# A two-layer encoder trunk on one core: gates and branch projections with token tiles as the stationary operand, and a transpose of the merged sum

## The chip, the core and the metric

The kernel runs on one core of one Trainium2 chip. Its metric is device time in microseconds (us). Three runs of the kernel before took 1342.67, 1344.53 and 1344.79 us; the median is 1344.53 us.

## What is computed

Two layers (`DEPTH = 2`) over 256 tokens of 1024 channels, all in float32. Each layer projects the tokens to three token mixers (pooling A, attention B, a gated recurrence C) and to three gates, projects the mixers' outputs to the model width, merges them by the gates and projects once more:

```
proj = einsum('bsd,de->bse', x, w_in[i])
...
y_a = einsum('bsc,cd->bsd', multiscale_pool(a_in, ...), w_branch_a[i])          # 1024 -> 1024
y_b = einsum('bsc,cd->bsd', dilated_attention_mixer(...), w_branch_b[i])        #  512 -> 1024
y_c = einsum('bsc,cd->bsd', hgrn2_bidirectional(...), w_branch_c[i])            # 1024 -> 1024
gates = sigmoid(gate_raw).reshape(B, S, 3, D_MODEL)
merged = gates[:, :, 0] * y_a + gates[:, :, 1] * y_b + gates[:, :, 2] * y_c
x1 = layer_norm(ALPHA * x + merged @ w_out[i], ln1_g[i], ln1_b[i])
```

A SwiGLU feed-forward, a gated per-layer embedding and a second layer norm end the layer.

## The kernel before

**Products.** Every matrix product is made of three matmuls per pair of tiles (`mm3`, L246 to L250): both operands are held as a high part and a low part of float32r, and high times high, high times low and low times high are added in PSUM. There are two ways to lay a product out. `gemm_cols` (L252) takes 128 weight columns as the stationary operand (`lhsT`) and moves all 256 tokens past them: 128x256 per matmul, and the result has output channels on the partitions. `gemm_tok` (L268) takes 128 tokens as the stationary operand and moves 512 weight columns: 128x512 per matmul, tokens on the partitions; it goes through both tiles of tokens (t = 0, 1), each with all eight tiles of k.

**The weight stream.** All weights come as 1 MB pieces in one fixed order, the list `chunks` (L139 to L176): `cols` is 256 columns of all eight k tiles, `blk` is 512 columns of four k tiles, `rws` 256 whole rows. A piece is loaded (`raw`, SP's queue, L193), split on ScalarE into `whi` (L206) and on VectorE into `wlo` (L207), and used. Each of the three names has three buffers, so the split of piece n waits until piece n-3 has been used by TensorE. `use_chunk` takes the next split piece; `step_end` (L241) splits one more piece and lets some background work be issued.

**Order.** The helper tasks of attention, recurrence and pooling are Python generators that are run in slices by `background` (L221). The order on each engine is then made by a scheduler over the whole program, so the program's text gives only dependences and priorities; the rows of the built program show the order itself.

**The stage in question**, L718 to L785, once in each layer. It makes, for branch C, four times a gate product (`gemm_cols` with the residual stream `xh`, `xl`), `gate` (tanh on ScalarE, L724) and the branch product (with `oh`, `ol`); VectorE then multiplies gate and product out of PSUM into `mg` (`merge`, L730). The pooling product follows (L747 to L757). Then branch B (half as deep) and its gates, and four times branch A's gate and product, where `merge` multiplies (L732) and adds (L733). `mg` has channels on the partitions, which is the layout that the output projection wants for its stationary operand: L782 and L783 split it into `mh`, `ml` as it is finished, a quarter at a time. The projection itself is `rows_gemm` (L799): four pieces of two k tiles, the first two pieces used at once for both tiles of tokens, the last two held and used tile by tile.

`tbank` gives one of four PSUM banks named `t` (transposes and small products), `gbank` one of four named `g`. `s4`, `s5`, `s7`, `s8`, `sa`, `sb` are named SBUF slots with one buffer each: a new tile in a slot waits for the last reader of the old one. A transpose is a matmul against `ident`.

Of the kernel before, what the change touches and what calls it, by code (L numbers as in the profile page):

```python
# [30 lines left out]
# columns of the constants' array  # L31
# [47 lines left out]
def trunk(ctx: ExitStack, tc: tile.TileContext, x, p, w_in, pool_w, pool_scale, w_branch_a,  # L79
# [59 lines left out]
    for l in range(DEPTH):  # L139
# [19 lines left out]
        for c in range(2):  # L159
            blk(w_branch_b[l], 0, 512 * c)  # L160
            cols(w_in[l], C_GATE + 1024 + 512 * c)
            cols(w_in[l], C_GATE + 1024 + 512 * c + 256)
        for c in range(4):
            cols(w_in[l], C_GATE + 256 * c)
            cols(w_branch_a[l], 256 * c)
# [75 lines left out]
    def step_end():  # L241
        split_chunk()
        background()

# [23 lines left out]
    def gemm_tok(ws, act, evac, between):  # L268
        """512 output columns, both tiles of tokens, ws: two pieces of four k tiles."""
        for t in range(2):  # L270
            ps = gbank()
            for k in range(KD):
                w = ws[k // 4]
                mm3(ps, act(k, t), (w[0][:, k % 4, :], w[1][:, k % 4, :]), k == 0, k == KD - 1)
# [37 lines left out]
    def layer_norm(t, gb, ress, then):  # L312
        """ress: per half of the columns (base, scale or None, psum)."""
# [29 lines left out]
    def hgrn_task(l, hp, q, ff, kf, fb, kb, vt, gt, oh, ol):  # L343
# [14 lines left out]
        for d in range(2):  # L358
# [30 lines left out]
            # totals of the chunks of 32  # L389
# [6 lines left out]
            # blocks of 64 stand at 0, 2, 4; the one scaled to its tile's far end beside the middle one  # L396
# [16 lines left out]
            # scaled: fwd queries block 3 by total of 2, keys block 0 by total of 1; bwd mirrored  # L413
# [130 lines left out]
    def pool_task(g, a, mix):  # L544
        # a: [P, 2, 272], the channels' values between zeros
# [88 lines left out]
    for l in range(DEPTH):  # L634
        # token-major operands: the recurrence's values and gate
# [51 lines left out]
        # attention  # L687
# [30 lines left out]
        # gates and branches  # L718
        finish("hgrn")
        mg = slot("s4", [P, KD, S])  # L720

        def gate(ps):
            s = misc([P, 512])
            A.activation(out=s, in_=ps, func=AF.Tanh, scale=0.5)  # L724
            return s

        def merge(s, y, c, first):
            dst = mg[:, 2 * c:2 * c + 2, :].rearrange("p m t -> p (m t)")
            if first:
                V.scalar_tensor_tensor(out=dst, in0=s, scalar=1.0, in1=y, op0=ALU.add, op1=ALU.mult)  # L730
            else:
                V.scalar_tensor_tensor(out=s, in0=s, scalar=1.0, in1=y, op0=ALU.add, op1=ALU.mult)  # L732
                V.tensor_tensor(out=dst, in0=dst, in1=s, op=ALU.add)  # L733

        for c in range(4):
            ps = gbank()
            gemm_cols(use_chunk(), xk, ps)
            s = gate(ps)
            step_end()
            ps = gbank()  # L740
            gemm_cols(use_chunk(), lambda k: (oh[:, k, :], ol[:, k, :]), ps)
            merge(s, ps, c, True)
            step_end()
# [15 lines left out]
        for c in range(2):  # L759
            pb = [gbank(), gbank()]  # L760
            w = use_chunk()
            for i in range(2):
                gemm_cols(w, lambda k: (ob[:, 0, k, :], ob[:, 1, k, :]), pb[i], nk=4, m0=2 * i)
            step_end()
            for i in range(2):
                ps = gbank()
                gemm_cols(use_chunk(), xk, ps)
                merge(gate(ps), pb[i], 2 * c + i, False)
                step_end()
        mh, ml = None, None  # L770
        for c in range(4):
            ps = gbank()
            gemm_cols(use_chunk(), xk, ps)
            s = gate(ps)
            step_end()
            ps = gbank()
# [142 lines left out]
```

## Time and profile before

| what | value |
|---|---|
| runs, us | 1342.67, 1344.53, 1344.79 (median 1344.53) |
| span of the profiled execution, us | 1341.4 |
| busy share of the span: TensorE, its weight loads, VectorE, ScalarE, GpSimd | 98%, 92%, 65%, 44%, 1% |
| granted TensorE clock, 40 slices | 9 tenths or more of full speed in every slice |
| mean DMA rate | 174 GB/s |

The profiled execution has no time of its own beside its span; the span starts and ends with the first and last instruction that the profiler shows, and the median of the runs is 3.1 us above it. A row of a timeline begins with its start in us and its length in us; a group of instructions has its count, its total busy time and the mean length of one in ns. A matmul's length is from its start to its modelled end and overlaps with the next one, so what a matmul costs in a row of them is the distance from start to start.

### The profile page before, as it was taken

To read this page: it belongs to the slowest core of one execution; us is meant where nothing else is said; L and a number is where in the kernel's file an instruction comes from. 1 tells how busy PE (TensorE), PEld (TensorE's weight loads), DVE (VectorE), ACT (ScalarE), POOL (GpSimd) and SP (SyncE) were. 2 spreads that over 40 slices of the span, in tenths; PEclk is the share of its full clock that TensorE was granted. 3 is DMA by queue.
4 is the path that set the end of the run, shared out by engine and by line. 5 is a ranking of instruction groups with operands and counts; after the bars stand their busy time and mean duration, and the time that the engine had idled before them with its cause. 6 is when DMAs were issued, how large, how long until landed. Compare 5 with 4: busy or idle time off the path is not lost.

```text
span 1341.4 us, 22091 instructions
## 1 busy us (share of the span) xinstructions
PE 1317.5 (98%) x9609; PEld 1236.9 (92%) x9609; DVE 868.7 (65%) x1126; ACT 585.9 (44%) x644; POOL 16.6 (1%) x24
## 2 busy tenths in 40 slices
PE   8999999999999999999989999999999999999997
PEld 6899999999999799998779999999999997999986
DVE  4598888574655765544555999875746558544545
ACT  5444444553444444443334444455534444444431
POOL 0000000000000000000000000000000000000000
PEclk9999999999999999999999999999999999999999
DMA  8654544245556465655356554442455564765551
GB/s 309 200 178 158 178 138 161 93 156 181 176 186 219 158 221 188 189 186 190 127 184 196 179 164 158 158 158 95 159 168 186 188 216 142 239 188 183 179 195 40
DMA packets 180769, 233.56 MB, mean 174 GB/s; under 512 B 3841, under 2 KB 149825, under 8 KB 180673
## 3 DMA queue, kind: packets, MB, share of 16 engines
q1 hardware_dynamic: 178976, 227.44, 51.7%
q10 hardware_dynamic: 1696, 4.72, 1.1%
q8 instruction: 75, 1.23, 0.4%
q14 instruction: 22, 0.17, 0.0%
HBM read 231.10 MB, written 1.05 MB: 173 GB/s over the span
## 4 chain that ended last, share of the span: by engine, by line
PE 93%; DVE 4%; issue 1%; ACT 1%; POOL 1%; DMA 0%; POOLq 0%; DVEq 0%; ACTq 0%
PE g L248 29%; PE g L249 28%; PE g L250 28%; DVE wlo L207 2%; PE t L439 1%; PE t L426 1%; PE t L434 1%; PE t L307 1%; POOL rs_y L297 1%; PE t L523 1%; PE t L463 1%; PE t L464 1%; ACT whi L206 0%; DVE ln_st L321 0%; PE t L503 0%
## 5 line engine op out<-in xcount | busy, mean ns | idle before, releaser
L207 DVE TENSOR_TENSOR wlo<-raw,whi 128x2048 fp32r<-128x2048 f32 (+2 forms) x218 | 489.9, 2248 | 339.7 <-ACT whi L206 339.4
L206 ACT ACTIVATE whi<-raw 128x2048 fp32r<-128x2048 f32 (+2 forms) x218 | 410.0, 1883 | 566.7 <-issue 259.6
L248 PE MATMUL g<-xh,whi 128*128 128x256 f32 x1984 | 564.4, 284 | 0.0
L250 PE MATMUL g<-xh,wlo 128*128 128x256 f32 x1984 | 561.7, 283 | 0.0
L249 PE MATMUL g<-xl,whi 128*128 128x256 f32 x1984 | 561.6, 283 | 0.0
L248 PEld LDWEIGHTS g<-xh,whi 128*128 128x128 f32 x1984 | 380.7, 192 | 0.2
L249 PEld LDWEIGHTS g<-xl,whi 128*128 128x128 f32 x1984 | 380.7, 192 | 0.2
L250 PEld LDWEIGHTS g<-xh,wlo 128*128 128x128 f32 x1984 | 380.6, 192 | 0.0
L248 PE MATMUL g<-whi,xh 128*128 128x512 f32 x288 | 115.1, 400 | 1.2 <-ACT whi L206 1.2
L249 PE MATMUL g<-wlo,xh 128*128 128x512 f32 x288 | 114.6, 398 | 1.4 <-DVE wlo L207 1.4
L250 PE MATMUL g<-whi,xl 128*128 128x512 f32 x288 | 113.3, 395 | 0.0
L249 PEld LDWEIGHTS g<-wlo,xh 128*128 128x128 f32 x288 | 55.6, 193 | 14.1 <-DVE wlo L207 3.1
L248 PEld LDWEIGHTS g<-whi,xh 128*128 128x128 f32 x288 | 55.6, 193 | 13.7 <-ACT whi L206 1.8
L250 PEld LDWEIGHTS g<-whi,xl 128*128 128x128 f32 x288 | 55.4, 192 | 11.5
L248 PE MATMUL g<-s,whi 128*128 128x256 f32 x192 | 54.3, 283 | 0.0
L250 PE MATMUL g<-s,wlo 128*128 128x256 f32 x192 | 54.3, 283 | 0.0
L249 PE MATMUL g<-s,whi 128*128 128x256 f32 x192 | 54.3, 283 | 0.0
L249 PE MATMUL g<-wlo,s 128*128 128x512 f32 x128 | 50.1, 392 | 0.0
L250 PE MATMUL g<-whi,s 128*128 128x512 f32 x128 | 50.1, 391 | 0.0
L248 PE MATMUL g<-whi,s 128*128 128x512 f32 x128 | 49.6, 390 | 0.0
L865 DVE TENSOR_TENSOR m<-m,g 128x512 f32<-128x512 f32 x22 | 15.1, 687 | 36.9 <-PE g L250 36.9
L248 PE MATMUL g<-whi,sa 128*128 128x512 f32 x96 | 37.5, 391 | 0.0
(177 smaller groups left out, 1472.4 us busy)
## 6 DMA issues: line engine op xcount, KB each, us to landing
raw<-in_w_in_dram SPq DMA_DIRECT2D x106, 1024.0 KB, 5.1
raw<-in_w_ffn_gate_dram SPq DMA_DIRECT2D x22, 1024.0 KB, 5.4
raw<-in_w_ffn_up_dram SPq DMA_DIRECT2D x22, 1024.0 KB, 5.4
raw<-in_w_ffn_down_dram SPq DMA_DIRECT2D x22, 1024.0 KB, 4.8
raw<-in_w_branch_c_dram SPq DMA_DIRECT2D x8, 1024.0 KB, 5.0
raw<-in_w_branch_a_dram SPq DMA_DIRECT2D x8, 1024.0 KB, 5.0
raw<-in_w_out_dram SPq DMA_DIRECT2D x8, 1024.0 KB, 4.8
raw<-in_w_ple_gate_dram SPq DMA_DIRECT2D x8, 1024.0 KB, 5.1
```

Source lines behind the costliest of these rows:

```text
L206: A.activation(out=hi[:, ks, :], in_=t[:, ks, :], func=AF.Copy)
L207: V.tensor_tensor(out=lo[:, ks, :], in0=t[:, ks, :], in1=f(hi[:, ks, :]), op=ALU.subtract)
L248: PE.matmul(ps, lhsT=ah, rhs=bh, start=first, stop=False)
L249: PE.matmul(ps, lhsT=ah, rhs=bl, start=False, stop=False)
L250: PE.matmul(ps, lhsT=al, rhs=bh, start=False, stop=last)
L297: G.tensor_tensor(out=y, in0=v, in1=mhalf.to_broadcast([P, n]) if n > 1 else mhalf, op=ALU.pow)
L307: PE.transpose(ps[:, k * P:(k + 1) * P], xt[:, t, (4 * hf + k) * P:(4 * hf + k + 1) * P], ident)
L426: PE.matmul(dg[po:po + 64, co:co + 64], lhsT=KI[:, cs], rhs=QI[:, cs], start=True, stop=True)
L434: PE.matmul(cr[po:po + 64, co:co + 64], lhsT=KL[:, h, 4 * t, :], rhs=QL[:, h, 4 * t, :], start=True, stop=True)
L439: PE.matmul(lg[:, co:co + P], lhsT=kp.rearrange("p b u -> p (b u)"), rhs=qp.rearrange("p b u -> p (b u)"), start=True, stop=True)
L463: PE.matmul(o, lhsT=at[:, 2 * h + t, :], rhs=vt[:, t, hs], start=True, stop=False)
L865: V.tensor_tensor(out=s, in0=s, in1=pu.rearrange("p (m t) -> p m t", t=S), op=ALU.mult)
```

## The change

The list of pieces has `blk` in place of `cols` for the gates and for branches A and C, and a new order of pieces. The stage's products go through `tok_block` (`gemm_tok` with one or two pieces): for each half n of the 1024 output columns a block of gate products and a block of branch products. Gates now stay in the slots s5 (branch C), s7 (B) and s8 (A) until the branch product is there. `mg` has tokens on the partitions. `turn(n)` transposes half n of it on TensorE, eight transposes in two banks, and splits the banks into `mh`, `ml`; `turn(0)` is a background task of branch A's second half, `turn(1)` is issued within `rows_gemm` after its first piece. The rest of the program has the same instructions. Helper lines move by a few: mm3's matmuls are L252 to L254, the split L210 and L211, the gate L728, merges L739, L741 and L742, the attention's transposes L528, their copy out of PSUM L530, its products with the values L536 to L539, pooling's split L296 and L297, the transposes of `p` L802, the new transposes L777 and their split L780 and L781.

```diff
-        for c in range(4):
-            cols(w_in[l], C_GATE + 2048 + 256 * c)
-            cols(w_branch_c[l], 256 * c)
+        for n in range(2):
+            for k in range(2):
+                blk(w_in[l], 512 * k, C_GATE + 2048 + 512 * n)
+            for k in range(2):
+                blk(w_branch_c[l], 512 * k, 512 * n)
...
-    def tok_block(act, evac, between=None):
-        ws = [use_chunk(), use_chunk()]
+    def tok_block(act, evac, between=None, n=2):
+        ws = [use_chunk() for _ in range(n)]
         gemm_tok(ws, act, evac, between)
-        step_end()
-        step_end()
+        for _ in range(n):
+            step_end()
...
-        mg = slot("s4", [P, KD, S])
+        mg = slot("s4", [P, 2, D])
...
+        def branch(n, gates, act, first=False, pieces=2, then=None):
+            def ev_gate(t, ps):
+                gate(ps, gates[:, t, :])
+            def ev(t, ps):
+                s, dst = gates[:, t, :], mg[:, t, 512 * n:512 * n + 512]
+                if first:
+                    V.scalar_tensor_tensor(out=dst, in0=s, scalar=1.0, in1=ps, op0=ALU.add, op1=ALU.mult)
+                else:
+                    V.scalar_tensor_tensor(out=s, in0=s, scalar=1.0, in1=ps, op0=ALU.add, op1=ALU.mult)
+                    V.tensor_tensor(out=dst, in0=dst, in1=s, op=ALU.add)
+            tok_block(xtok, ev_gate)
+            tok_block(act, ev, n=pieces)
...
+        def turn(n):
+            for j in (2 * n, 2 * n + 1):
+                ps = tbank()
+                for k in range(2):
+                    for t in range(2):
+                        c0 = (2 * j + k) * P
+                        PE.transpose(ps[:, k * S + t * P:k * S + (t + 1) * P], mg[:, t, c0:c0 + P], ident)
+                ks = slice(2 * j, 2 * j + 2)
+                v = ps.rearrange("p (k t) -> p k t", t=S)
+                A.activation(out=mh[:, ks, :], in_=v, func=AF.Copy, scale=0.5)
+                V.scalar_tensor_tensor(out=ml[:, ks, :], in0=v, scalar=0.5, in1=f(mh[:, ks, :]),
+                                       op0=ALU.mult, op1=ALU.subtract)
...
-        rows_gemm(4, 2, lambda k, t: (mh[:, k, t * P:(t + 1) * P], ml[:, k, t * P:(t + 1) * P]), ln1)
+        finish("turn")
+        rows_gemm(4, 2, lambda k, t: (mh[:, k, t * P:(t + 1) * P], ml[:, k, t * P:(t + 1) * P]), ln1,
+                  lambda: turn(1))
```

The order on the engines is the scheduler's, and it changes at two places that matter below; both are of the first layer, and the second layer has the same.

TensorE, where branch C begins (before; `m` is a tile of attention probabilities, `sa`, `sb` are `oh`, `ol`):

```order
L250 MATMUL g<-xh,wlo 128x256
L523 MATMUL t<-ident,m 128x128 x8
L248 MATMUL g<-sa,whi 128x256
L249 MATMUL g<-sb,whi 128x256
L250 MATMUL g<-sa,wlo 128x256
...
L531 MATMUL t<-m,s_455 128x128
L532 MATMUL t<-m,s_455 128x128
L533 MATMUL t<-m,s_455 128x128
L534 MATMUL t<-m,s_456 128x128
```

The same place after the change:

```order
L528 MATMUL t<-ident,m 128x128 x8
L252 MATMUL g<-whi,sa 128x512
L536 MATMUL t<-m,s_455 128x128
L537 MATMUL t<-m,s_455 128x128
L538 MATMUL t<-m,s_455 128x128
L539 MATMUL t<-m,s_456 128x128
...
L253 MATMUL g<-wlo,sa 128x512
L254 MATMUL g<-whi,sb 128x512
```

Before, all 48 matmuls of a branch product stood between the attention's transposes and the products that read the transposed probabilities; now there is one.

ScalarE at that place after the change (`s_3005` is a tile of gates, `m<-t` the copy of the transposed probabilities out of PSUM):

```order
L728 ACTIVATE s_3005<-g 128x512
L210 ACTIVATE whi<-raw 128x2048
L293 ACTIVATE h<-h 128x512
L728 ACTIVATE s_3005<-g 128x512
L530 ACTIVATE m<-t 128x512 x2
L210 ACTIVATE whi<-raw 128x2048
```

The two copies stand right behind the second gate tile of the block.

TensorE, where the merged sum is transposed and the output projection begins (after the change; the first eight transposes are between branch A's last gate block and its last product block, the last eight behind the first piece of the output projection):

```order
L254 MATMUL g<-whi,xl 128x512
L777 MATMUL t<-ident,s_3004 128x128 x8
L252 MATMUL g<-whi,s_3336 128x512
...
L802 MATMUL t<-ident,s_3892 128x128 x4
L252 MATMUL g<-whi,sa 128x512
...
L777 MATMUL t<-ident,s_3004 128x128 x8
L252 MATMUL g<-whi,sa 128x512
```

Before, only the four transposes of `p` (L795) stood there.

## Rows read from the trace of the kernel before

**Rows 1.** The page: the span, busy time of each engine, two of the lines over 40 equal slices (tenths of a slice), and the chain of work that ended last, by engine.

```profile
span 1341.4 us, 22091 instructions
PE 1317.5 (98%) x9609; PEld 1236.9 (92%) x9609; DVE 868.7 (65%) x1126; ACT 585.9 (44%) x644; POOL 16.6 (1%) x24
...
PE   8999999999999999999989999999999999999997
...
PEclk9999999999999999999999999999999999999999
...
PE 93%; DVE 4%; issue 1%; ACT 1%; POOL 1%; DMA 0%; POOLq 0%; DVEq 0%; ACTq 0%
```

**Rows 2.** The waits of TensorE's matmuls over the whole span: us in total, times, longest.

```profile
PE t L307 <- DVE x L332: 7.5, 6, 3.5
...
PE g L249 <- DVE wlo L207: 1.4, 1, 1.4
```

**Rows 3.** Engines in stretches of the span: from the gates and branches of the first layer (352 to 424 us), from the second layer's first token-major blocks (690 to 719) and from one of its blocks with strided tokens (738 to 748). Columns: length, then busy time and count of PE, PEld, DVE, ACT, POOL, granted clock, DMA share, GB/s.

```profile
352.00:424.00 72.00, 72.00 (x602) 72.00 (x602) 40.23 (x31) 29.66 (x24) 0.00 (x0) 1.00 0.56 190
...
690.00:719.00 29.00, 29.00 (x130) 24.01 (x129) 13.44 (x8) 13.66 (x12) 0.00 (x0) 1.00 0.67 217
738.00:748.00 10.00, 10.00 (x44) 8.28 (x44) 10.00 (x17) 4.98 (x5) 0.00 (x0) 1.00 0.58 197
```

**Rows 4.** TensorE's timeline, first and last row of 630 matmuls of form 128x256 in a row, in the gates and branches of the first layer.

```profile
350.50 0.28 PE L248 MATMUL g<-s,whi 128*128 128x256 f32 x1
...
425.99 0.28 PE L250 MATMUL g<-s,wlo 128*128 128x256 f32 x1
```

**Rows 5.** TensorE's timeline, first and last row of 141 matmuls of form 128x512 in a row: token-major blocks (`gemm_tok` with `xtok`) of the second layer.

```profile
688.37 0.39 PE L248 MATMUL g<-whi,xh 128*128 128x512 f32 x1
...
720.11 0.39 PE L250 MATMUL g<-whi,xl 128*128 128x512 f32 x1
```

**Rows 6.** TensorE's timeline, first and last row of 48 matmuls of form 128x512 in a row: a block of the second layer whose tokens are taken with a stride of two (`xperm`).

```profile
737.60 0.39 PE L248 MATMUL g<-whi,xh 128*128 128x512 f32 x1
...
748.56 0.40 PE L250 MATMUL g<-whi,xl 128*128 128x512 f32 x1
```

**Rows 7.** TensorE's timeline at the beginning of branch C, first layer: eight transposes between matmuls of form 128x256.

```profile
296.47 0.28 PE L250 MATMUL g<-xh,wlo 128*128 128x256 f32 x1
296.59 1.04 PE L523 MATMUL t<-ident,m 128*128 128x128 f32 x8
297.38 0.36 PE L248 MATMUL g<-sa,whi 128*128 128x256 f32 x1
297.59 0.28 PE L249 MATMUL g<-sb,whi 128*128 128x256 f32 x1
```

**Rows 8.** TensorE's timeline where attention's probabilities meet the values: the first of one set of four lines, and the instruction behind the set; each line runs in two passes.

```profile
281.53 0.39 PE L531 MATMUL t<-m,s 128*128 128x128 f32 x2
...
282.43 0.38 PE L503 MATMUL t<-h 128*128 128x256 f32 x1
```

**Rows 9.** ScalarE's timeline at the beginning of branch C, first layer: the gate, a weight split, the copies of the transposed probabilities.

```profile
296.85 0.60 ACT L724 ACTIVATE m<-g 128x512 f32<-128x512 f32 x1 [1.93 <-PE g L250]
297.35 1.91 ACT L206 ACTIVATE whi<-raw 128x2048 fp32r<-128x2048 f32 x1
299.15 1.07 ACT L525 ACTIVATE m<-t 128x512 f32<-128x512 f32 x2
```

**Rows 10.** ScalarE's timeline in the token-major blocks of the second layer.

```profile
696.05 1.92 ACT L206 ACTIVATE whi<-raw 128x2048 fp32r<-128x2048 f32 x1 [2.12 <-PE g L250]
698.77 0.60 ACT L640 ACTIVATE s<-g 128x512 f32<-128x512 f32 x1 [0.80 <-PE g L250]
...
706.93 1.92 ACT L206 ACTIVATE whi<-raw 128x2048 fp32r<-128x2048 f32 x1 [2.12 <-PE g L250]
709.65 0.60 ACT L649 ACTIVATE m<-g 128x512 f32<-128x512 f32 x1 [0.80 <-PE g L250]
```

**Rows 11.** VectorE's timeline in the same blocks.

```profile
698.00 2.29 DVE L207 TENSOR_TENSOR wlo<-raw,whi 128x2048 fp32r<-128x2048 f32 x1 [4.93 <-ACT whi L206]
...
708.88 2.29 DVE L207 TENSOR_TENSOR wlo<-raw,whi 128x2048 fp32r<-128x2048 f32 x1 [3.35 <-ACT whi L206]
711.09 0.68 DVE L650 TENSOR_TENSOR s<-g,m 128x512 f32<-128x512 f32 x1
```

**Rows 12.** Groups of instructions, shapes apart: count, busy us, mean ns of one, idle time before them.

```profile
L724 ACT ACTIVATE m<-g 128x512 f32<-128x512 f32 x32 | 18.7, 585 | 18.3 <-PE g L250 18.3
...
L733 DVE TENSOR_TENSOR s<-s,m 128x512 f32<-128x512 f32 x16 | 11.1, 693 | 0.6
...
L732 DVE SCALAR_TENSOR_TENSOR m<-m,g 128x512 f32<-128x512 f32 x16 | 10.9, 683 | 13.4 <-PE g L250 13.4
...
L783 DVE SCALAR_TENSOR_TENSOR sb<-s,sa 128x512 fp32r<-128x512 f32 x8 | 5.5, 684 | 0.0
...
L782 ACT ACTIVATE sa<-s 128x512 fp32r<-128x512 f32 x8 | 4.9, 614 | 0.0
```

**Rows 13.** TensorE's timeline at the end of branch A, first layer: the transposes of `p` right behind the last branch matmul, the output projection's first matmuls.

```profile
426.11 0.60 PE L795 MATMUL t<-ident,s 128*128 128x128 f32 x4
426.46 0.48 PE L248 MATMUL g<-whi,sa 128*128 128x512 f32 x1
426.77 0.39 PE L249 MATMUL g<-wlo,sa 128*128 128x512 f32 x1
```

More of the change, by code (lines that the diff above doesn't have):

```diff
@@ L268, in gemm_tok @@
     def gemm_tok(ws, act, evac, between):
+        nk = 4 * len(ws)
         for t in range(2):
             ps = gbank()
-            for k in range(KD):
+            for k in range(nk):
                 w = ws[k // 4]
-                mm3(ps, act(k, t), (w[0][:, k % 4, :], w[1][:, k % 4, :]), k == 0, k == KD - 1)
+                mm3(ps, act(k, t), (w[0][:, k % 4, :], w[1][:, k % 4, :]), k == 0, k == nk - 1)
                 if t == 0 and k == 5 and between is not None:
@@ L719, in trunk, with gate, tok_of @@
         finish("hgrn")
-        mg = slot("s4", [P, KD, S])
-        def gate(ps):
-            s = misc([P, 512])
+        mg = slot("s4", [P, 2, D])
+        def gate(ps, s):
             A.activation(out=s, in_=ps, func=AF.Tanh, scale=0.5)
             return s
[L727 to L743, printed above, removed]
+        def branch(n, gates, act, first=False, pieces=2, then=None):
[10 more added lines that the diff above has]
+            tok_block(act, ev, n=pieces)
+        def tok_of(hi, lo):
+            return lambda k, t: (hi(k)[:, t * P:(t + 1) * P], lo(k)[:, t * P:(t + 1) * P])
+        for n in range(2):
+            branch(n, slot("s5", [P, 2, 512]), tok_of(lambda k: oh[:, k, :], lambda k: ol[:, k, :]), first=True)
         finish("attn1")
@@ L758, in trunk @@
         step_end()
[L759 to L776, printed above, removed]
-            gemm_cols(use_chunk(), lambda k: (ph[:, k, :], pl_[:, k, :]), ps)
-            merge(s, ps, c, False)
-            if mh is None:
-                mh, ml = slot("sa", [P, KD, S], F32R), slot("sb", [P, KD, S], F32R)
-            ks = slice(2 * c, 2 * c + 2)
-            A.activation(out=mh[:, ks, :], in_=mg[:, ks, :], func=AF.Copy, scale=0.5)
-            V.scalar_tensor_tensor(out=ml[:, ks, :], in0=mg[:, ks, :], scalar=0.5, in1=f(mh[:, ks, :]),
-                                   op0=ALU.mult, op1=ALU.subtract)
-            step_end()
@@ new lines, in trunk @@
+        for n in range(2):
+            branch(n, slot("s7", [P, 2, 512]), tok_of(lambda k: ob[:, 0, k, :], lambda k: ob[:, 1, k, :]), pieces=1)
+        mh, ml = slot("sa", [P, KD, S], F32R), slot("sb", [P, KD, S], F32R)
+        def turn(n):
+            for j in (2 * n, 2 * n + 1):
+                ps = tbank()
+                for k in range(2):
+                    for t in range(2):
[6 more added lines that the diff above has]
+                                       op0=ALU.mult, op1=ALU.subtract)
@@ L788, in trunk, with turn_later @@
+        def turn_later(n):
+            yield None
+            turn(n)
+            yield 2000
+        for n in range(2):
+            branch(n, slot("s8", [P, 2, 512]), tok_of(lambda k: ph[:, k, :], lambda k: pl_[:, k, :]))
+            if n == 0:
+                tasks.append(("turn", turn_later(0)))
         pT = slot("s7", [P, 2, S])
@@ L797, in trunk, with rows_gemm @@
         gb = load_gb("s5", ln1_g[l], ln1_b[l])
-        def rows_gemm(n, late, act, base):
+        def rows_gemm(n, late, act, base, between=None):
             banks = [[gbank(), gbank()], [gbank(), gbank()]]
@@ L814, in rows_gemm @@
                     part(i, w, 1)
+                    if i == 0 and between is not None:
+                        between()
                     step_end()
@@ L848, in ev @@
             def ev(t, ps):
-                s = gate(ps)
+                s = gate(ps, misc([P, 512]))
                 V.scalar_tensor_tensor(out=s, in0=s, scalar=1.0, in1=pl2[:, t, cs], op0=ALU.add, op1=ALU.mult)
```

15 lines of the change are left out of this document (8 added, 7 removed).

## The prediction

> **What bounds the kernel now.** I read the page first, then TensorE's waits, then its timeline in the stage that is changed. The page shows TensorE busy for 98% of the span, at full granted clock in every slice, and 93% of the chain that ended last is TensorE's own work [rows 1]. Of its waits none of the larger ones belongs to the gates and branches: the longest, 7.5 us in six waits, is for the layer norms' output, and the one for a split weight is a single wait of 1.4 us [rows 2]. In a stretch of 72 us inside the changed stage TensorE is busy for all 72.00 us, with VectorE at 40.23, ScalarE at 29.66 and the DMA engines at 0.56 [rows 3]. So in this stage the time is TensorE's matmuls, start to start, and nothing else. An instruction added to TensorE there is paid in full; one added to ScalarE or VectorE costs nothing until it makes TensorE wait.
>
> What counts is therefore the distance from start to start. For the form that the stage uses now, 256 tokens moving, it is (425.99 - 350.50) / 629 = 120.0 ns [rows 4]. For 512 weight columns moving, with token tiles of the same residual stream as the still operand, it is (720.11 - 688.37) / 140 = 226.7 ns [rows 5]. Where the tokens are taken with a stride it is (748.56 - 737.60) / 47 = 233.2 ns [rows 6]. The granted clock reads 1.00 in all three stretches, the 2.4 GHz level [rows 3], so these distances can be compared. Two narrow matmuls cost 240.0 ns, one wide one that does the same work 226.7: 13.3 ns are saved each time.
>
> **The change, part by part.**
>
> The products. One layer has gates of 3 x 1024 columns, branches A and C of 1024 and B of half that depth. In narrow matmuls that is 3 x 192 + 192 + 192 + 96 = 1056, in wide ones 528. The gain is 1056 x 120.0 - 528 x 226.7 = 126.7 - 119.7 = 7.0 us in a layer, **14.0 us** in both. The ends: with the distance of the strided blocks, 233.2, it would be 7.2 us in all; a distance below 226.7 shows nowhere in these rows. I take 226.7, because the still operands of the new blocks are contiguous slices of 128 tokens, as in the blocks at that distance [rows 5].
>
> Here one page of the Trainium skill differs from the trace. "TensorE: Matmul & The Clock Gate" (section "Wait — 56ns, not 53.3ns?") gives a fixed cost of about 2.5 ns per matmul beside one column per cycle at 2.4 GHz. By it narrow and wide would take 109.2 and 215.8 ns and both layers would gain only 2.6 us. The trace does not agree: it leaves 13.3 ns per matmul [rows 4, 5].
>
> The transposes. Each layer has two new groups of eight on TensorE. Such a group stands in the trace at the beginning of branch C: from the last matmul ahead of it to the second behind it are 297.59 - 296.47 = 1.12 us [rows 7], where two narrow distances alone would be 0.24; a group costs 0.88 us. The four transposes of `p` give the same by another way: 426.77 - 425.99 [rows 4, 13] less one narrow and one wide distance is 0.43 us for four. Nothing hides them, since TensorE has no idle time here: 4 x 0.88 = **+3.5 us**.
>
> Work that only changes place. There are as many gates, merges and splits of the merged sum as before, on tiles of the same size: 0.585 us for a gate, 0.683 and 0.693 for a merge, 0.614 and 0.684 for a split [rows 12]. The splits now read PSUM; the merge that reads PSUM takes 0.683 us and the one that reads SBUF 0.693 [rows 12], so I change nothing. Number and size of the weight pieces, and the loads on SP's queue, stay. All this is hidden behind TensorE as long as it is on time; three places decide that.
>
> First, **attention's last products**. The order shows that only one matmul now stands between the transposed probabilities and the products that read them, where 48 stood. With T the start of the last gate matmul: the gate of the second tile starts 0.38 us after its last matmul's start [rows 7, 9], some 0.1 later for the longer row of a wide one (0.39 against 0.28) [rows 4, 5], and the next ScalarE instruction 0.50 later [rows 9], so the two copies run from T + 1.0, 1.07 us together [rows 9]; the first ends at T + 1.5. TensorE spends 0.23 on the last matmul, 0.79 on the transposes [rows 7] and 0.3 on the one matmul, and asks for the copy at T + 1.3: it waits 0.2 us. The first set of products takes 0.90 us [rows 8], so the second copy is ready for the second set. **+0.4 us** in two layers. The lower end is no wait. The upper one is a weight split of 1.91 us [rows 9] that is still running ahead of the gate: 2.1 us a layer, 4.2 in all.
>
> Second, **the second half of a block's weights**. A block holds two of the three buffers, so the second piece of the next block can be split only when the first piece of this one has been used for both tiles of tokens, at three quarters of the block. The existing blocks show just that [rows 10, 11]: `whi` starts at 696.05, `wlo` ends at 698.00 + 2.29 = 700.29. The next block starts at 688.37 + 45 x 0.2267 = 698.57 and needs it 12 matmuls later, at 701.29: on time by 1.0 us. One block later it ends at 711.17 for 712.17, again 1.0. A layer has six such places in the new stage (three in branch C, three in branch A; behind branch B's short blocks the buffers come free earlier). The merges do not lie across them: two take 1.38 us [rows 12] from about 0.4 us after half a block, while `wlo` waits for three quarters plus 1.9 us. I take no cost.
>
> Third, **the second group of transposes**, behind the first piece of the output projection. VectorE's queue after the last branch matmul, at T: a `wlo` that ends about T + 1.6 (its buffer came free 2.7 us before T, then 1.92 and 2.29), the multiply, a `wlo` whose buffer comes free at T and that ends about T + 4.6, the add; the sum is ready at about T + 5.3. TensorE arrives at T + 0.2 + 0.4 + 24 x 0.2267 = T + 6.1. That is on time by 0.8 us; if the cover is gone, each us late is paid twice, once a layer. Behind it ScalarE splits weights before it reads the transposed banks, but the held pieces, which need them, begin a whole piece (5.4 us) later.
>
> The sum: -14.0 + 3.5 + 0.4 = **-10.1 us**. Against the profiled span of 1341.4 us that is 1331.3; the median of the runs is 3.1 us above the span, and I leave that distance: 1344.5 - 10.1 = **1334.4 us**.
>
> **The rivals.**
>
> (a) *The wide distance here is that of the busy blocks.* The blocks at 233.2 ns differ from those at 226.7 in their stride, but also in VectorE being busy for all of 10.00 us, against 13.44 of 29 [rows 3]. If the load and not the stride makes the difference, and the new stage has it, the gain is 7.2 - 3.5 - 0.4 = 3.3 us: 1341.2. Against it: VectorE is busy for 40.23 of 72 us in this stage, nearer to the quiet blocks. Chance 0.07.
>
> (b) *Slower: the second halves come late.* Mechanism: at the twelve places above TensorE stands still at the quarter of a block, because the split pair has lost its 1.0 us of room to gates and merges queued ahead of it. If each is late by d beyond that, 12 d is paid. It outweighs the sum from d = 0.84 us, and makes the kernel measurably slower (0.2%, 2.7 us, about what a measurement of this kernel can tell from no change) from d = 1.07, that is from splits 2.1 us later than in the existing blocks [rows 10, 11]; at d = 1.1 the time is 1347.5. For it: branch A puts two merges per tile on VectorE where the existing blocks have one operation of 0.68 [rows 11]. Against it: the order of work worked out above. Chance 0.05.
>
> (c) *The 13.3 ns are not a cost per matmul.* Then a wide matmul costs 2 x 120.0 ns in this stage, the products gain nothing, and the transposes and the wait remain: +3.9 us, 1348.4. For it: no wide block in the trace has gates or branches in it. Against it: both wide stretches of the trace are below 240. Chance 0.03. By the page's 2.5 ns the sum would be -2.6 + 3.5 + 0.4 = +1.3 us, 1345.8 and no difference to be seen; the measured distances [rows 4, 5] speak against it in the same way.
>
> (d) *Attention's copies are late by a whole split.* 4.2 us in place of 0.4: 1338.2. Chance 0.03.
>
> That the change does not do what it says I can leave out: the order shows the wide forms, the transposes and the new places.
>
> **How the numbers follow.** The forecast has 0.82 and its own range. Its low end is the sum with no wait at attention, -10.5, and runs as far below their median as the lowest of before (1.9): 1332.0. Its high end takes rival (d) and 0.1 us at each of the twelve places, -14.0 + 3.5 + 4.2 + 1.2 = -5.1: 1339.5. Rivals (a), (b) and (c) lie outside, 0.15 together. Faster by over 0.2%, that is below 1341.8: the forecast, (d) and a part of (a), which lies at the bound: 0.88. Within 0.2%: the rest of (a), small cases of (b) and (c): 0.06. Slower: 0.06.
>
> **What would show it right or wrong.** In the changed profile: 1056 more matmuls of form 128x512 and 2112 fewer of 128x256; a distance of 226 to 228 ns in the stage's blocks; 32 more transposes, each group of eight about 0.9 us; no wait for `wlo` in the stage, and one wait of some 0.2 us for L530 at the beginning of branch C in each layer; a span near 1331. The prediction is wrong if the blocks run at 233 or more, if waits for `wlo` add up to several us, or if TensorE waits at L777 for the last add.

## The result, and the profile after

The changed kernel takes 1334.03 us (median of 4 runs, 1333.53 to 1334.69), the kernel before 1343.68 beside it (4 runs): ratio 0.9929, 95% interval 0.9916 to 0.9941, or -9.65 us. The forecast was 1334.4. A second set of five runs of the same changed kernel gave 1333.27 (label a0_change_again below), ratio 0.9921 [0.9907, 0.9935], -10.4 us.

The page of the changed kernel answers to [rows 1]: matmul records fall from 9609 to 8585, which is -2112 + 1056 + 32. The span falls from 1341.4 to 1332.6, TensorE's share of it stays at 98%, weight loads fall from 92% to 89%, and the clock's line now has one slice at 8 tenths, to which I come back.

```profile
span 1332.6 us, 20047 instructions
PE 1308.5 (98%) x8585; PEld 1185.8 (89%) x8585; DVE 867.5 (65%) x1126; ACT 587.1 (44%) x644; POOL 16.7 (1%) x24
...
PEclk9999999999999999999989999999999999999999
...
PE 93%; DVE 4%; ACT 1%; issue 1%; POOL 1%; DMA 0%; POOLq 0%; DVEq 0%; ACTq 0%
```

A stretch of the changed stage in the first layer, with the columns of [rows 3]. TensorE is still busy all the time, 306 matmuls in 68 us where 602 stood in 72; the weight loads, which filled the whole stretch before, now take 56.40 of 68.00.

```profile
352.00:420.00 68.00, 68.00 (x306) 56.40 (x305) 37.95 (x29) 29.30 (x22) 0.00 (x0) 1.00 0.59 203
```

TensorE's timeline there, the first and the last row of 278 wide matmuls in a row, and the first new group of transposes, `turn(0)`. The distance is (408.30 - 345.48) / 277 = 226.8 ns, that of the existing wide blocks [rows 5]. From 408.30 to the second matmul behind the group, at 409.64, are 1.34 us; two wide distances make 0.454 of that, so the group costs 0.89.

```profile
345.48 0.40 PE L253 MATMUL g<-wlo,xh 128*128 128x512 f32 x1
...
408.30 0.39 PE L254 MATMUL g<-whi,xl 128*128 128x512 f32 x1
408.54 1.03 PE L777 MATMUL t<-ident,s 128*128 128x128 f32 x8
409.32 0.48 PE L252 MATMUL g<-whi,s 128*128 128x512 f32 x1
409.64 0.40 PE L253 MATMUL g<-wlo,s 128*128 128x512 f32 x1
```

The beginning of branch C, answering to [rows 7, 9]: TensorE, then ScalarE. Attention's transposes now have one matmul between them and the products that read them (L536).

```profile
301.58 0.39 PE L254 MATMUL g<-whi,xl 128*128 128x512 f32 x1
301.81 1.03 PE L528 MATMUL t<-ident,m 128*128 128x128 f32 x8
302.60 0.48 PE L252 MATMUL g<-whi,sa 128*128 128x512 f32 x1
303.15 0.49 PE L536 MATMUL t<-m,s 128*128 128x128 f32 x2
303.48 0.39 PE L537 MATMUL t<-m,s 128*128 128x128 f32 x2
```

```profile
302.01 0.60 ACT L728 ACTIVATE s<-g 128x512 f32<-128x512 f32 x1 [0.23 <-PE g L254]
302.50 1.08 ACT L530 ACTIVATE m<-t 128x512 f32<-128x512 f32 x2
```

From 301.58 to 303.15 are 1.57 us where 1.34 would be without a wait, and the first line of L536 takes 0.33 to the next one instead of the 0.22 of its fellows: about 0.33 us in all. In the waits of TensorE's weight loads over the whole span (us in total, times, longest) it stands in the first row below; two of its four, 0.2 us each, are of another place and stood in the kernel before too (second row). The two rows behind them are of the changed kernel's matmuls: the single wait for `wlo` is the one of [rows 2], at 664 us, near the end of the first layer. In the stretch from 290 to 480 us no wait for `wlo` is listed, on either.

```profile
PEld t L536 <- ACT m L530: 1.2, 4, 0.4
```

```profile
PEld t L531 <- ACT m L525: 0.5, 2, 0.2
```

```profile
PE t L312 <- DVE x L337: 7.7, 6, 3.5
...
PE g L253 <- DVE wlo L211: 1.4, 1, 1.4
```

The second new group, `turn(1)`, behind the first piece of the output projection: VectorE's last add (L742), then TensorE. The sum is ready at 424.79 + 0.68 = 425.47 and TensorE comes to it at 426.22.

```profile
422.59 2.29 DVE L211 TENSOR_TENSOR wlo<-raw,whi 128x2048 fp32r<-128x2048 f32 x1
424.79 0.68 DVE L742 TENSOR_TENSOR s<-s,s 128x512 f32<-128x512 f32 x1
```

```profile
425.99 0.40 PE L254 MATMUL g<-whi,sb 128*128 128x512 f32 x1
426.22 1.03 PE L777 MATMUL t<-ident,s 128*128 128x128 f32 x8
427.01 0.47 PE L252 MATMUL g<-whi,sa 128*128 128x512 f32 x1
427.33 0.39 PE L253 MATMUL g<-wlo,sa 128*128 128x512 f32 x1
```

**Two marks that make the traces comparable.** Spans of two executions differ by more than the terms in question, so I take two intervals. A runs from the recurrence's first row of sixteen small products (`t<-w`, L431; L426 before) to the second layer's first layer-norm transposes (`t<-ident,x`, L312; L307 before) and holds the first layer's changed stage. Its ends in the kernel before, the changed kernel and its repetition are these rows of TensorE's timeline:

```profile
88.76 0.69 PE L426 MATMUL t<-w 128*64 128x64 f32 x16
...
679.25 0.99 PE L307 MATMUL t<-ident,x 128*128 128x128 f32 x5 [3.47 <-DVE x L332]
```

```profile
88.81 0.69 PE L431 MATMUL t<-w 128*64 128x64 f32 x16
...
674.42 1.97 PE L312 MATMUL t<-ident,x 128*128 128x128 f32 x8 [3.47 <-DVE x L337]
```

```profile
88.97 0.69 PE L431 MATMUL t<-w 128*64 128x64 f32 x16
...
674.53 1.97 PE L312 MATMUL t<-ident,x 128*128 128x128 f32 x8 [3.47 <-DVE x L337]
```

B is the same for the second layer: from the first two transposes of `w` there (755.46 us in the kernel before, 751.54 in the changed one, 750.36 in its repetition) to the end of the span. The span is given to 0.1 us, so B and its differences are good to about 0.1. All runs in these two intervals, and their median times:

| kernel | A, us | B, us | A and B against a0 | median, us |
|---|---|---|---|---|
| before | 590.49 | 585.94 | +4.93, +5.00 | 1343.68 |
| the change | 585.61 | 581.06 | +0.05, +0.12 | 1334.03 |
| a0_change_again | 585.56 | 580.94 | | 1333.27 |
| e1_width256 | 592.47 | 587.89 | +6.91, +6.95 | 1347.95 |
| e2_width128 | 697.33 | | +111.77 | 1556.2 |
| e9_width192_320 | 603.00 | | +17.44 | 1369.46 |
| e3_transposes_twice | 587.33 | 582.67 | +1.77, +1.73 | 1337.03 |
| e4_no_transposes | 583.76 | 579.07 | -1.80, -1.87 | 1330.27 |
| e5_split_plus_quarter | 585.71 | 581.23 | +0.15, +0.29 | 1333.78 |
| e6_split_plus_three_quarters | 587.87 | 583.28 | +2.31, +2.34 | 1337.82 |
| e8_attention_earlier | 585.23 | 580.62 | -0.33, -0.32 | 1333.35 |
| e7_ffn_wide | 583.74 | 579.07 | -1.82, -1.87 | 1329.95 |
| e10_ffn_wide_attention_earlier | 583.41 | 578.70 | -2.15, -2.24 | 1328.54 |

The two executions of the changed kernel agree in A to 0.05 us and in B to 0.12. The change is worth 4.88 to 5.00 us per layer. e2 and e9 were run once each, the others four to six times.

### The profile page after: what moved, and what is told of

Read it like the earlier page. It is cut to its first block, busy times and chain, and to the rows that moved or that the text cites. A ratio compares the mean times of both kernels' runs of the same rounds, so it can differ in the third digit from the quotient of the medians.

```text
span 1332.6 us, 20047 instructions
## 1 busy us (share of the span) xinstructions
PE 1308.5 (98%) x8585; PEld 1185.8 (89%) x8585; DVE 867.5 (65%) x1126; ACT 587.1 (44%) x644; POOL 16.7 (1%) x24
## 4 chain that ended last, share of the span: by engine, by line
PE 93%; DVE 4%; ACT 1%; issue 1%; POOL 1%; DMA 0%; POOLq 0%; DVEq 0%; ACTq 0%
PE g L252 28%; PE g L253 28%; PE g L254 28%; DVE wlo L211 2%; PE t L444 1%; PE t L431 1%; PE t L439 1%; PE t L312 1%; POOL rs_y L302 1%; PE t L468 1%; PE t L469 1%; ACT whi L210 0%; DVE ln_st L326 0%; PE t L508 0%; PE t L528 0%
## 5 line engine op out<-in xcount | busy, mean ns | idle before, releaser
L211 DVE TENSOR_TENSOR wlo<-raw,whi 128x2048 fp32r<-128x2048 f32 (+2 forms) x218 | 489.8, 2249 | 347.4 <-ACT whi L210 347.0
L210 ACT ACTIVATE whi<-raw 128x2048 fp32r<-128x2048 f32 (+2 forms) x218 | 409.9, 1883 | 517.5 <-issue 220.7
L252 PE MATMUL g<-xh,whi 128*128 128x256 f32 x1600 | 455.6, 285 | 0.0
L254 PE MATMUL g<-xh,wlo 128*128 128x256 f32 x1600 | 453.1, 283 | 0.0
L253 PE MATMUL g<-xl,whi 128*128 128x256 f32 x1600 | 453.0, 283 | 0.0
L252 PEld LDWEIGHTS g<-xh,whi 128*128 128x128 f32 x1600 | 307.0, 192 | 0.2
L253 PEld LDWEIGHTS g<-xl,whi 128*128 128x128 f32 x1600 | 307.0, 192 | 0.2
L254 PEld LDWEIGHTS g<-xh,wlo 128*128 128x128 f32 x1600 | 306.9, 192 | 0.0
L252 PE MATMUL g<-whi,xh 128*128 128x512 f32 x480 | 190.2, 397 | 1.3 <-ACT whi L210 1.2
L253 PE MATMUL g<-wlo,xh 128*128 128x512 f32 x480 | 189.5, 395 | 1.4 <-DVE wlo L211 1.4
L254 PE MATMUL g<-whi,xl 128*128 128x512 f32 x480 | 188.1, 393 | 0.0
L252 PEld LDWEIGHTS g<-whi,xh 128*128 128x128 f32 x480 | 91.8, 191 | 21.2 <-ACT whi L210 1.8
L254 PEld LDWEIGHTS g<-whi,xl 128*128 128x128 f32 x480 | 91.6, 191 | 19.1
L254 PE MATMUL g<-whi,s 128*128 128x512 f32 x224 | 87.5, 390 | 0.0
L252 PE MATMUL g<-whi,s 128*128 128x512 f32 x224 | 87.1, 390 | 0.0
L252 PE MATMUL g<-whi,sa 128*128 128x512 f32 x160 | 62.8, 393 | 0.0
L254 PE MATMUL g<-whi,sb 128*128 128x512 f32 x160 | 62.3, 389 | 0.0
L254 PEld LDWEIGHTS g<-whi,s 128*128 128x128 f32 x224 | 42.0, 188 | 8.6
```

Source lines behind the costliest of these rows:

```text
L210: A.activation(out=hi[:, ks, :], in_=t[:, ks, :], func=AF.Copy)
L211: V.tensor_tensor(out=lo[:, ks, :], in0=t[:, ks, :], in1=f(hi[:, ks, :]), op=ALU.subtract)
L252: PE.matmul(ps, lhsT=ah, rhs=bh, start=first, stop=False)
L253: PE.matmul(ps, lhsT=ah, rhs=bl, start=False, stop=False)
L254: PE.matmul(ps, lhsT=al, rhs=bh, start=False, stop=last)
```

## Experiments

**a0_change_again.** The changed kernel itself, measured beside e1, e3 and e4 as their base. Below, "on a0" is the difference to its median.

> The changed kernel once more, beside the kernel before, as the reference for the other runs. Expected: 10 us below the kernel before (ratio 0.9925), no wait for wlo inside the gates and branches, and at the end of layer 1 a stretch at the lower clock level whose length may differ from one execution to the next by about 1 us.

Measured: 1333.27 us (1332.71 to 1333.59), beside 1343.71 of the kernel before (11 runs).

**e1_width256.** All of the change, but each wide matmul moves its 512 columns as twice 256 past the same still operand; the first matmul of each bank stays whole.

```diff
+    def mm3_narrow(ps, a, b, first, last, width):
...
+        parts = [slice(c, c + width) for c in range(0, 512, width)]
...
+            for cs in parts:
+                PE.matmul(ps[:, cs], lhsT=lhs, rhs=rhs[:, cs], start=False, stop=end and cs is parts[-1])
...
-            tok_block(xtok, ev_gate)
+            tok_block(xtok, ev_gate, width=256)
```

> All as in the change (token tiles as the still operand, same pieces, same transposes), but each matmul of the new blocks except the first of its bank moves 256 weight columns instead of 512, twice: 1008 matmuls of 512 columns become 2016 of 256. Theory, a cost per matmul of 13.3 ns beside its columns: 1008 x 13.3 = 13.4 us slower than the change, that is 3 to 4 us slower than the kernel before. Rival, the gain comes from the exchanged roles of the operands and not from the number of matmuls: no difference to the change, 10 us faster than before. With a cost per matmul of 2.5 ns it would be 2.5 us slower than the change.

Measured: 1347.95 us (1346.70 to 1348.57), ratio to before 1.0029 [1.0018, 1.0040], so slower than before, with every other part of the change in place. TensorE's timeline (rows of two matmuls) has them at (351.56 - 350.12) / 12 = 120.0 ns:

```profile
350.12 0.40 PE L281 MATMUL g<-whi,xl 128*128 128x256 f32 x2
350.36 0.40 PE L281 MATMUL g<-whi,xh 128*128 128x256 f32 x2
...
351.56 0.40 PE L281 MATMUL g<-whi,xl 128*128 128x256 f32 x2
```

That is 504 x 13.2 = 6.7 us per layer, and A and B show 6.9. Of the 0.2 to 0.3 us per layer that are left, about 0.2 is at the first matmul of a bank, which stays whole: the next one starts 236 ns behind it (mean of 22 of the first layer's 24) where wide ones start 227 apart. The median is 14.7 us above a0, the span 15.2; 1.26 of the span's difference lies between A and B, at the layer boundary (told of at the end of the next section). The gain is thus in the width, that is in the number of matmuls, and not in which operand stands still. One page of the Trainium skill, "TensorE: Matmul & The Clock Gate" (section "Wait — 56ns, not 53.3ns?"), would have the split cost its 2.5 ns per matmul, an estimate of 1.3 us per layer; the run does not agree.

**e2_width128** and **e9_width192_320.** The same edit with four parts of 128, and with parts of 192 and 320.

> As the run with 256 columns, but with 128 columns per matmul, four in place of each wide one. If the cost per matmul is a constant 13.3 ns: 128/2.4 + 13.3 = 66.6 ns from start to start, four for 226.7, 1008 x 39.7 = 40 us slower than the change. If a lower bound per matmul, as in the trace's transposes and attention products of this width (0.10 to 0.11 us each), comes first: four for 0.40 to 0.44 us, 175 to 216 us slower.

> The wide blocks of gates and branches moved as 192 and 320 columns in place of 512 (the first matmul of a bank stays whole), 504 matmuls of a layer split. Theory: a matmul costs the larger of a floor of about 0.1115 us (the distance at 128 columns in the run before) and its columns at one per cycle plus 13.3 ns; so 0.1115 + 0.1467 = 0.258 us in place of 0.2268: +15.8 us per layer. Rival: no floor but a smooth rise from 0.1115 us at 128 columns to 0.120 at 256, which makes 0.1158 at 192: +18.0 us per layer. A second rival, that the 13.3 ns are a cost per matmul at every width and the floor at 128 was something else: 0.0933 + 0.1467 = 0.240 us, +6.7 us per layer as with 2 x 256.

Measured, one run each: 1556.2 us, and 1369.46 us. The timelines (rows of four, and of two matmuls, one of either width):

```profile
349.74 0.61 PE L281 MATMUL g<-whi,xh 128*128 128x128 f32 x4
...
351.97 0.50 PE L281 MATMUL g<-whi,xl 128*128 128x128 f32 x3
```

```profile
352.07 0.43 PE L281 MATMUL g<-whi,xh 128*128 128x192 f32 x2
...
352.85 0.42 PE L281 MATMUL g<-whi,xh 128*128 128x192 f32 x2
```

The same place of e9 seen from within a pair, so that its second matmul, the one of 320 columns, has a row of its own:

```profile
352.16 0.34 PE L281 MATMUL g<-whi,xh 128*128 128x320 f32 x1
352.33 0.42 PE L281 MATMUL g<-wlo,xh 128*128 128x192 f32 x2
```

A matmul of 128 columns takes (351.97 - 349.74) / 20 = 111.5 ns, hardly less than one of 256; a pair of 192 and 320 takes 0.78 / 3 = 260 ns. So the 13.3 ns beside the columns hold at 256 and 512 columns only, and a constant 13.3 at every width (40 us in e2, 6.7 us per layer in e9) is refuted by both runs. e2 lies 222.9 us above a0, a little over the 175 to 216 expected, since the 0.10 to 0.11 us that they were worked out from became 0.1115. In e9 the sum of a pair lies between the theory's 258 ns (+15.8 us per layer) and the rival's 262.5 (+18.0), and A shows +17.4. Its parts fit neither: the 320 columns start 0.09 us behind the 192, and the next 192 start 0.17 behind the 320, where both accounts have 0.11 to 0.12 and then 0.15. So 0.11 us is what a matmul of 128 columns takes in a row of its kind and not a floor under every distance below 256; that the expected sum came near was luck, and what sets the distances between stays open. The section "Back-to-back issue gap" of the same page of the Trainium skill has some 81 ns at 128 columns and 131 at 512 for a stream of load and matmul; for these float32r products the trace has 111.5 and 226.8, and does not agree.

In a stretch of e2's stage the weight loads are busy 143.35 of 145.00 us (PEld is the second engine), as they are all the time at 256 columns [rows 3], and only 56.40 of 68.00 at 512. That fits loads of the still operand as what holds the narrow forms up, but no run here loads once for two matmuls, so it is not shown.

```profile
355.00:500.00 145.00, 144.26 (x1272) 143.35 (x1271) 45.71 (x37) 34.30 (x30) 0.00 (x0) 1.00 0.34 112
```

**e3_transposes_twice.** Each new transpose is done twice, into the same place.

```diff
-                for k in range(2):
+                for k in [0, 1] * 2:
                     for t in range(2):
...
                         PE.transpose(ps[:, k * S + t * P:k * S + (t + 1) * P], mg[:, t, c0:c0 + P], ident)
```

> Every transpose of the merged sum is made twice into the same place. Theory, nothing hides them: 4 groups of 8 more, 0.88 us each, 3.5 us slower than the change; the second group in each layer still comes after the sum is ready. Rival, the transposes are hidden in the space that waits leave (0.3 us a layer at most in the trace): under 1 us slower.

Measured: 1337.03 us (1336.35 to 1338.12), ratio 0.9949 [0.9937, 0.9962], +3.8 us on a0, and +1.77 and +1.73 per layer. The group of sixteen in its timeline:

```profile
408.49 0.40 PE L254 MATMUL g<-whi,xl 128*128 128x512 f32 x1
408.72 1.91 PE L777 MATMUL t<-ident,s 128*128 128x128 f32 x16
410.39 0.47 PE L252 MATMUL g<-whi,s 128*128 128x512 f32 x1
410.70 0.39 PE L253 MATMUL g<-wlo,s 128*128 128x512 f32 x1
```

2.21 less two wide distances is 1.76 us: 0.11 us each, with no fee for the group.

**e4_no_transposes.** The split reads the merged sum without turning it.

```diff
-                ps = tbank()
...
-                        PE.transpose(ps[:, k * S + t * P:k * S + (t + 1) * P], mg[:, t, c0:c0 + P], ident)
...
-                v = ps.rearrange("p (k t) -> p k t", t=S)
+                v = mg[:, j % 2, 512 * n:512 * n + 512].rearrange("p (k t) -> p k t", t=S)
```

> The transposes of the merged sum are left out: the split reads the merged sum as it lies in SBUF, so the output projection gets it in the wrong layout (the result is not the reference's). Everything else stands. Theory: 3.5 us faster than the change, and the products' gain alone is seen against the kernel before: 14.0 less 0.4, 13.6 us faster. Rival, hidden transposes: under 1 us faster than the change.

Measured: 1330.27 us (1329.42 to 1330.87), ratio 0.9898 [0.9885, 0.9912], -3.0 us on a0; by A and B -1.80 and -1.87 per layer, -3.7 in both. From both sides the transposes cost 3.5 to 3.7 us.

**e5_split_plus_quarter** and **e6_split_plus_three_quarters.** Does VectorE's work have room in the stage? Before each `wlo` of the stage a part of it is computed once more, 0.69 us in e5, about 1.75 in e6 (the edit of e6; e5 has `k * 1 // 4`).

```diff
+            if i in stage:
+                es = slice(0, k * 3 // 4)
+                V.tensor_tensor(out=lo[:, es, :], in0=t[:, es, :], in1=f(hi[:, es, :]), op=ALU.subtract)
```

> VectorE makes a quarter of each weight split of the changed stage twice: 0.69 us more for every piece. Theory, the second half of a block's weights is on time by about 1.0 us: within 1 us of the change, no wait for wlo in the stage. Rival, the room is already used up by gates and merges: 12 places x 0.69 = 8 us slower than the change.

> VectorE makes three quarters of each weight split of the changed stage twice: about 1.75 us more for every piece. Theory, 1.0 us of room at twelve places: TensorE waits 0.75 us at each, 9 us slower than the change (about as slow as the kernel before), with the waits for wlo at the thirteenth matmul of the blocks that follow a full block. Rival, the room is much larger than computed: no difference to the change. VectorE then has about 9.5 us of work in a block of 10.9, so single places may be later.

Measured: e5 1333.78 us (1333.10 to 1333.95), ratio 0.9928 [0.9913, 0.9943], as the change (A and B have +0.15 and +0.29), with no wait for `wlo` listed in the stage; e6 1337.82 us (1337.24 to 1338.37), ratio 0.9958 [0.9941, 0.9974], +4.5 us on a0, half of what I expected. The waits of e6's weight loads from 290 to 480 us (first row), and the longest, in TensorE's matmuls:

```profile
PEld g L259 <- DVE wlo L217: 2.9, 6, 1.1
```

```profile
342.55 0.50 PE L259 MATMUL g<-wlo,xh 128*128 128x512 f32 x1 [0.62 <-DVE wlo L217]
```

There are six waits in the layer, and A and B show 2.3 us per layer where I expected six times 0.75. That there are as many as the places that I counted is chance. Four stand at counted places (branch C's second gate and product, branch A's first product and second gate). The other two are in branch B, where VectorE has fallen behind, and the longest of all, the row above, is one of these, at the first piece of B's first gate. The scheduler also made TensorE's order anew: in branch C's second product of e6 the matmul that waits is the 16th of its block, where in the changed kernel the first one to read the second piece's `wlo` is the 14th, so others fill a part of the wait. So e6 shows that this much more work is no longer hidden, but not how large the room was.

The room can be read in the changed kernel itself, here in branch C's second product, on VectorE and on TensorE (the 14th matmul of the block):

```profile
326.08 2.29 DVE L211 TENSOR_TENSOR wlo<-raw,whi 128x2048 fp32r<-128x2048 f32 x1 [5.84 <-ACT whi L210]
```

```profile
329.55 0.39 PE L253 MATMUL g<-wlo,sa 128*128 128x512 f32 x1
```

The split is ready at 328.37 and read at 329.55: 1.2 us of room. It is 1.2 at all four of these places, 4.2 at branch C's first product and 2.1 at branch A's second; at the first piece of B's first gate, which I did not count, it is 1.35.

e6 also bears on rival (a). In a stretch of it VectorE is busy all the time (columns of [rows 3]), and the wide matmuls there start (385.98 - 373.96) / 53 = 226.8 ns apart, 54 in a row:

```profile
374.00:386.00 12.00, 12.00 (x55) 9.93 (x54) 12.00 (x9) 3.73 (x3) 0.00 (x0) 1.00 0.72 229
```

```profile
373.96 0.39 PE L258 MATMUL g<-whi,s 128*128 128x512 f32 x1
...
385.98 0.39 PE L260 MATMUL g<-whi,xl 128*128 128x512 f32 x1
```

**e8_attention_earlier.** Background work may be issued within branch C's first gate block, so attention's transposes come half a block earlier.

```diff
-            tok_block(xtok, ev_gate)
+            tok_block(xtok, ev_gate, background if first and n == 0 else None)
```

> Background work may also be issued within the first gate block of branch C, so attention's last transposes come in the middle of that block, 24 or more wide matmuls ahead of the products that read them. Theory: the wait for the copy out of PSUM (0.3 us in each layer in the trace of the change) goes, 0.6 us in all, too little to be told by the times; it is read from the trace. Rival: the copy then stands behind a weight split and something else waits.

Measured: 1333.35 us (1332.87 to 1333.56), ratio 0.9925 [0.9911, 0.9940]; the median cannot tell it from a0. The trace can: -0.33 and -0.32 us per layer, and the wait for L530 is gone, L536 starts one wide distance after the last gate matmul:

```profile
303.00 0.39 PE L254 MATMUL g<-whi,xl 128*128 128x512 f32 x1
303.23 0.38 PE L536 MATMUL t<-m,s 128*128 128x128 f32 x2
```

**e7_ffn_wide** and **e10_ffn_wide_attention_earlier.** What the prices say of the feed-forward: its gate and up projections turned too, the product of both transposed on TensorE; e10 adds e8's edit.

```diff
+        for c in range(NF // 4):
+            ss = [misc([P, 512]), misc([P, 512])]
...
+            tok_block(xtok, ev_silu)
+            tok_block(xtok, ev_up)
+            tasks.append(("turn", turn_hidden(c, ss)))
```

> The feed-forward's gate and up projections are turned the same way too: for all but the last 256 hidden columns the tokens stand still and 512 weight columns move, which makes 960 narrow matmuls of a layer 480 wide ones; the product of the two is transposed on TensorE, 40 transposes of 128 x 128 more per layer. My theory (a matmul costs its columns plus about 13.3 ns, a transpose in a row 0.11 us, nothing waits longer): -480 x 13.3 ns = -6.4 us and +40 x 0.11 = +4.4 us per layer, so -4 us in two layers against the change, 1329.3 us beside the change's 1333.3. A rival, that the feed-forward's weights come late once whole 512-column chunks are wanted at once (their second halves, with up to 1 us each at 20 places): -4 + up to 20 = up to 1349. A second rival, that the transposes stand waiting for the multiplication (about 0.7 us on DVE at each of 10 places): 1333 to 1336.

> Two edits of earlier runs together: the feed-forward's gate and up projections turned too, and attention's transposes half a block earlier. If the two do not touch each other: 1329.9 us of the first alone less 2 x 0.33 us, the price of the wait by the trace of the second alone: 1329.3 us. If the earlier background step costs the later blocks something: 1330 or more.

Measured: e7 1329.95 us (1329.58 to 1330.33), ratio 0.9899 [0.9882, 0.9915]; per layer -1.82 and -1.87 for -2.0 expected. e10 1328.54 us (1328.15 to 1328.60), ratio 0.9887 [0.9871, 0.9904], the fastest of all; by A and B the second edit is worth -0.33 and -0.37 per layer on top, as it is alone. e7's median is 0.65 us above the expected 1329.3; e10's is 0.8 below its own 1329.3. By the prices worked out ahead of e7, the forty transposes per layer cost 4.4 of the 6.4 us that the products gain; the run shows only what is left, 1.8 to 1.9.

## Why the prediction was right

- **What bounds.** TensorE's starts were the time of the stage before and are after: 68.00 of 68.00 us busy. No term came from another engine but the one at attention. TensorE has one more wait for a split weight than the working names, 1.2 us for `whi` at 6.8 us of the span; it is far from the stage.
- **The products, -14.0.** 1056 x 120.0 - 528 x 226.8 = 7.0 us per layer, with the distance read in the changed stage itself; e1 undoes just this and takes it back. Rival (a), 233.2 ns, fell: the distance is that of the quiet blocks, with VectorE busy for 37.95 of 68 us. Its mechanism fell too: with VectorE busy all the time in e6 the distance is still 226.8. That the stride makes the 233.2 is what remains; no run tried it. Rival (c) fell by the same distance and by e1. The chance of 0.03 for it was fair, as every wide stretch in the trace spoke against it.
- **The transposes, +3.5.** 0.89 us per group in the trace, 1.76 for sixteen in e3, 3.0 to 3.8 us in all by the medians of e4 and e3.
- **Attention's wait, +0.4.** 0.33 us per layer by the trace and by e8, where I had 0.2. The working gave the wait itself right (0.23) and left out that the first product behind it stands 0.11 longer before the next. Rival (d) did not come about: no weight split ran ahead of the gate.
- **The second halves, 0.** No wait; e5 shows that 0.69 us more on VectorE cost nothing that the median shows, e6 that 1.75 us more do. The working's room of 1.0 us was 0.2 too small: it takes twelve distances to the matmul that reads the late `wlo`, but that one is the 14th of its block, thirteen distances in. The working also counts two places that have more room, and leaves out the first piece of branch B's first gate, where e6 waits longest. Rival (b) needed waits from splits that come 2.1 us later; nothing in the stage comes near that.
- **The second group, 0.** On time by 426.22 - 425.47 = 0.75 us, with 0.8 forecast.

Per layer -7.0 + 1.77 + 0.33 = -4.9 us, and A and B have -4.88 to -5.00; the forecast, -5.05 per layer.

That 1334.03 lies within 0.4 us of 1334.4 is in part luck: the kernel before took 1343.68 beside it, 0.85 less than the 1344.53 that the forecast starts from. The differences, -9.65 and -10.4, lie 0.3 to 0.5 us to either side of the -10.1. Three results of the working are off by a tenth (the range's ends should be 1332.1 and 1339.4, rival (b)'s time 1347.6); nothing hangs on it.

**What the profile's span leaves over.** It fell by 8.8 and not by 10.1. A and B give -9.76; the other 0.96 stand outside, 0.91 of it between the two intervals, from 679.25 to 755.46 before (76.21 us) and from 674.42 to 751.54 after (77.12). There TensorE has idled for 3.47 us ahead of the layer norm's transposes, and the granted clock is low behind that. The ten us from that start on, in the kernel before, the changed one and its repetition (columns of [rows 3]):

```profile
679.25:689.25 10.00, 9.98 (x39) 7.87 (x40) 3.65 (x4) 4.02 (x5) 0.00 (x0) 0.83 0.11 41
```

```profile
674.42:684.42 10.00, 10.00 (x35) 8.21 (x36) 2.76 (x4) 3.12 (x3) 0.00 (x0) 0.70 0.09 36
```

```profile
674.53:684.53 10.00, 10.00 (x41) 8.34 (x42) 4.05 (x4) 4.40 (x5) 0.00 (x0) 0.83 0.10 37
```

The mean granted clock is 0.70 in the first execution of the changed kernel and 0.83 in the second, as before; the same program takes 77.12 and 75.83 us over this part. All thirteen traces divide in this way: in four the mean clock of these ten us is 0.69 to 0.73, and the part between the intervals takes 76.80 to 77.20 us; in the nine others, the kernel before among them, it is 0.83, and the part takes 75.83 to 76.32. So it is a spread between executions and no part of the change; why one execution has the longer stretch at the lower level no run shows. In the repetition the whole span is 10.1 us below the one of before.

## What to carry to other kernels

Where TensorE is back to back, price a layout by its start-to-start distances: here 120.0 ns for 256 columns and 226.8 for 512, so halving the number of matmuls gives 13.3 ns per pair, and a transpose that it makes necessary costs 0.11 us, as much as eight such pairs save. Below 256 columns this price does not hold. The turn pays where one transpose serves many products (528 pairs for 16 transposes per layer here; 480 for 40 in the feed-forward, which still gained 1.8 us per layer). For effects below the spread of the runs, compare marks within the traces: they repeat to 0.1 us where medians of the same kernel differ by 0.8. And where a scheduler orders the whole program, an edit to one engine's work can move another engine's instructions, as e6 did; compare the orders before reading a wait as a price.

## What was not expected of the hardware

A matmul of 128 columns takes 111.5 ns beside 120.0 for 256 columns, both at a granted clock of 1.00: halving 256 columns saves 7%. A transpose of 128 x 128 in a row takes 0.11 us too; whether for the same reason was not tried. A matmul of 192 columns is followed after 0.09 us and one of 320 after 0.17 when they take turns, so neither distance alone is columns plus a constant. And after the same idle time of 3.47 us, the low clock lasted differently long in two executions of one program, for a difference of 1.3 us.
